# Modulation blocks of gated linear attention: eight fillers of four loads, or thirty single loads and two behind the scores of its units

## The chip, the cores and the metric

The kernel runs on one core of a Trainium2 chip. The metric is device time in microseconds (us) from one execution of the whole program. All work is single precision in and out; large products are split into a high and a low part of a narrower format (`F32R`), so that each is three matmuls.

## What is computed

Two transformer blocks, one behind the other, on 512 tokens of width 1024. What matters here lies in the first:

```python
def adaln_params(cond, w_mod, b_mod):
    return jnp.split(jax.nn.silu(cond) @ w_mod + b_mod, 6, axis=-1)
...
        sh1, sc1, gt1, sh2, sc2, gt2 = [m[:, None, :] for m in adaln_params(c, w_mod[l], b_mod[l])]
...
        qg, kg, vg, r, gf, gb = gla_inputs(px, gla_gate_up[l], gla_gate_bias[l])
        _, _, og = gla_bidir(qg, kg, vg, gf, gb, s_f, s_b)
...
        od = diff_attend(qd, jnp.concatenate([kd_c, kd], axis=2), jnp.concatenate([vd_c, vd], axis=2), lam)
        mix = jnp.concatenate([gla_merge(og, r, gla_norm_g[l]), diff_merge(od, diff_norm_g[l], lam_init)], axis=-1) @ w_out[l]
        x = x + gt1 * mix
        x = x + gt2 * swiglu(modulate(x, norm2_g[l], sh2, sc2), w_ffn_in[l], w_ffn_out[l])
```

`sh1` and `sc1` are needed at the very start. The other four modulation vectors (`gt1`, `sh2`, `sc2`, `gt2`: 4096 columns of `w_mod`, 16.8 MB) are needed only behind both attentions. The gate `r` is needed in `gla_merge`.

## The kernel before, in words

The stretch at issue has two stages. **Gated linear attention** (some 187 to 323 us of the trace) is a loop over 16 units (4 chunks of 128 tokens by 4 heads). A unit is `out_exp` (matmuls L834 to L839 that sum gates, then exponentials on ACT), `out_ops` (DVE multiplies L857 to L861 that scale queries and keys), `out_scores` (matmuls L873 to L883, copies and a masked sum on ACT and DVE up to L895) and `out_unit` (matmuls L903 and L904). The loop writes the scores of unit u, then `out_exp` and `out_ops` of unit u + 1, then `out_unit` of u. At the head of a chunk `xgates` computes the next chunk's gates (L782). **Differential attention** (some 323 to 480 us) loops over 4 heads by 4 query tiles; its first matmuls are the transposes L958, its scores L998 and L999.

Both stages have short matmuls with chains through ACT and DVE between them. To keep TensorE (PE) busy, independent work is written between them from a list, `fillers`. Each entry has a cost, and `fill_in(us)` takes entries while the time granted covers half the cost of the next. A unit grants `FG` = 4.2 us, a query tile `FA` = 3.2 us. The list holds tiles of the projections `w_dk`, `w_dv` and `w_dq` (cost 2.9, 24 matmuls L285 to L287 of 256 columns), four tiles of the gate projection `w_gr` (cost 5.5, 24 matmuls L196 to L198 of 512 columns, then a sigmoid on ACT, L147 to L149), for the memory of the second block `mem_in` (eight pieces, L1058 and on), `mem_stats`, `mem_k` and `mem_v`, and, at the places `GM` and `MM`, eight modulation blocks (cost 3.9).

A **modulation block** makes 512 of the 4096 columns. It loads 2 MB as four pieces `wm` of 512 KB (L680) and issues eight matmuls L332 (`acc<-wm,silc`), two to a piece. They have 32 output rows each, and go in turn to four strips of TensorE, so that four can run side by side. Then ACT copies the sum (L335, `mr`), four transposes follow (L338), and DVE adds up (L339, L341). Four blocks are fillers of the loop, four of differential attention.

Pieces `wm` and all weight tiles `wf` share one ring of two buffers. Weights that are loaded there (L178) leave their buffer when ACT has made the high part (L187, `whi`) and DVE the low part (L188, `wlo`); these parts have three buffers each. A `wm` leaves when its matmuls are done. All these loads are issued by SP, in order; a load that waits for its buffer holds up those behind it. Accumulators `acc` have two PSUM banks. A scheduler at build time merges the work into one fixed order for each engine; every engine then runs its list in order.

Of the kernel before, what the change touches and what calls it, by code (L numbers as in the profile page):

```python
# [10 lines left out]
F32 = mybir.dt.float32  # L11
# [8 lines left out]
KT = D // 128  # L20
# [7 lines left out]
NLEV = 7  # L28
RW = 1088
GH = 0  # L30
FA, FG, FC, A0, GM, AM, AP = 3.2, 4.2, 6.5, 2, (25, 28, 31, 34), 0, ()
PJ, FP = 10, 8
NF = 2
T0 = 1
T1 = 3
NP = 3
FS = 0.6
MM = (0, 2, 4, 6)
NR = 1
GV = 0  # L40
PL = 3
# [40 lines left out]
def kernel(ctx: ExitStack, tc: tile.TileContext, a: dict, out: bass.AP, stop=None):  # L82
    nc = tc.nc
    V, G, A, T = nc.vector, nc.gpsimd, nc.scalar, nc.tensor
# [5 lines left out]
    ring = ctx.enter_context(tc.tile_pool(name="ring", bufs=3))  # L90
# [8 lines left out]
    def acc():  # L99
        return ps.tile([128, 512], F32, tag="acc", name="acc", bufs=naccs)  # L100
# [19 lines left out]
    silc = const.tile([128, KT, 32], F32, name="silc")  # L120
# [98 lines left out]
    def fm(w, ms, nk, bhi, blo, alloc, evac, segs=FULL, lo_eng=None, after=None, keep=None, every=4,  # L219
           have=None):  # L220


        def chunk(m, k0):
            if nk == 4:
                hi, lo = wsplit(w[m // 2].rearrange("p m k c -> p (m k c)"), 1024, lo_eng, keep and keep())
                have[m + 1, 0] = hi[:, 512:], lo[:, 512:]
                return hi, lo
            kn = min(8, nk - k0)
            return wsplit(w[m, :, k0:k0 + kn, :].rearrange("p k m -> p (k m)"), kn * 128, lo_eng, keep and keep())

        have = {} if have is None else have
        for a_, b_ in segs:
            for m in ms:
                p = alloc(m)
                for k in range(nk):
                    c = (m, k // 8)
                    if c not in have:
                        have[c] = chunk(m, k // 8 * 8)
                    hi, lo = have[c]
                    sl = slice(k % 8 * 128, k % 8 * 128 + 128)  # L240
                    mm3(p[:, a_:b_], hi[:, sl], lo[:, sl], bhi(k)[:, a_:b_], blo(k)[:, a_:b_], k == 0, k == nk - 1)
                    if k % every == every - 1 and k < nk - 1:
                        step()
                evac(m, a_, b_, p[:, a_:b_])
                step()
            if len(segs) > 1:
                drain()
                if after is not None:
                    between.append(after(a_, b_))
# [71 lines left out]
    mid2 = mid.enter_context(tc.tile_pool(name="mid2", bufs=2))  # L321
    X0 = midp.tile([128, KT, S], F32, tag="a16", name="X0")

    def mod_block(m0, n, load, mpool):


        p = acc()[:, :128 * n]
        for k in range(KT):
            if k == 0 or (k - k0 + 1) * 128 * n > wf.shape[-1]:
                wf, k0 = load(k), k  # L330
            j = k % 4
            ins = T.matmul(p[32 * j:32 * j + 32, :], silc[:, k], wf[:, (k - k0) * 128 * n:(k - k0 + 1) * 128 * n],  # L332
                           start=k < 4, stop=k >= 4, skip_group_check=True, tile_position=(0, 32 * j)).ins
        mr = mpool.tile([128, 128 * n], F32, tag="mr", name="mr")
        A.copy(mr, p)  # L335
        q = acc()[:, :128 * n]
        for i in range(n):
            T.transpose(q[:, i * 128:(i + 1) * 128], mr[:, i * 128:(i + 1) * 128], ident)  # L338
        V.tensor_reduce(mods[:, m0:m0 + n], q.rearrange("p (m j r) -> p m r j", m=n, j=4)[:, :, 0:2, :], AX, ALU.add)  # L339
        o = COLS["b_mod"][0] + m0  # L340
        V.tensor_tensor(mods[:, m0:m0 + n], mods[:, m0:m0 + n],  # L341
                        cols[:, o:o + n].rearrange("p (m o) -> p m o", o=1).to_broadcast([128, n, 2]), ALU.add)
        return ins

    def affine(dst, gname, sc0, row, k0=0, kn=KT):

# [16 lines left out]
    with tc.tile_pool(name="st", bufs=1) as st, tc.tile_pool(name="st2", bufs=2) as st2:  # L363
# [84 lines left out]
        ins = mod_tiles(8)  # L448
        warm(WV, ins)
        nx = normed(X0, S, "x")  # L450
        ins = next(nx)
# [14 lines left out]
        ins = mod_tiles(10)  # L466
        for k0 in (2, 4, 6):
            ins = queued(ins, lambda: next(part))
            ins = queued(ins, lambda: mod_tiles(k0))
# [4 lines left out]
            ins = queued(ins, lambda: next(part))  # L474
            if k0 < 6:
                ins = queued(ins, lambda: mod_tiles(10 + k0))
# [5 lines left out]
        if Q3:  # L482
            ins = queued(ins, lambda: next(part))
# [5 lines left out]
        for _ in range(2 - Q3):  # L489
            ins = queued(ins, lambda: next(part))  # L490
# [65 lines left out]
    for t in range(2):  # L556
        p = acc()
# [8 lines left out]
    for dst, t0, n in ((downc[0:32, :], 0, 2), (down[0:32, 1:1 + S], 2, 4)):  # L566
        p = mis()
# [50 lines left out]
    fillers = []  # L618
# [49 lines left out]
    def silu_r(m, x, y, p):  # L668
# [2 lines left out]
        e = mid2.tile([128, S], F32, tag="sg", name="sg", bufs=1)  # L671
        sigmoid(e, p)
        V.tensor_tensor(got_rs[0][:, m], p, e, ALU.mult)
    for m in range(4):
        fillers.append((5.5, lambda m=m: fm(a["w_gr"], [m], KT, hx, hxl, accs, silu_r)))

    def mod_job(n):
        def load(k):
            t = ring.tile([128, RW], F32, tag="wf", name="wm", bufs=2)[:, :1024]
            nc.sync.dma_start(t, a["w_mod"][n, k // 4, :, k % 4:k % 4 + 2].rearrange("p k n -> p (k n)"))  # L680
            return t
        return lambda: mod_block(16 + 4 * n, 4, load, mid2)
    mod_jobs = [(3.9, mod_job(n)) for n in range(8)]
    for at in GM:
        fillers.insert(at, mod_jobs.pop(0))
    left = [0.0]
    late_by = [0]

    def fill_in(us):

        left[0] += us
        while fillers and left[0] >= 0.5 * fillers[0][0]:
            cost, run = fillers.pop(0)
            pe_late[0] = late_by[0]
            run()
            pe_late[0] = 0
            left[0] -= cost
# [43 lines left out]
    for jt in range(2):  # L741
        pe = s2()[:, :512]
        for z, ldiag in ((0, LSUF), (1, LPX)):
# [6 lines left out]
            for i, (lm, t) in enumerate(terms):  # L750
                for r, gx in enumerate(cg[t][1:]):
                    T.matmul(zsl(pe, z), Lr[:, lm], zsl(gx, z), start=i == 0 and r == 0,
                             stop=i == len(terms) - 1 and r == 1, skip_group_check=True)
# [34 lines left out]
    for c in range(TT):  # L788
# [7 lines left out]
        for h in range(4):  # L796
            T.matmul(pe[:, 512 + 32 * h:544 + 32 * h], g[:, h * 128:(h + 1) * 128], f32(Lr[:, LONE, 0:32]), start=True, stop=True,
                     skip_group_check=True)
# [26 lines left out]
    def out_exp(c, h):  # L825

        if h == GH and c < 3:
            gx[c + 1] = xgates(c + 1, 1)
        g, gh, gl = gx[c]
        hs = slice(h * 128, (h + 1) * 128)  # L830
        pe = s2()
        for j in range(4):
            b = slice(32 * j, 32 * j + 32)
            T.matmul(pe[b, 896:1024], g[:, hs][:, b], f32(Lr[:, LPRE if j < 2 else LSUF]), start=True, stop=True,  # L834
                     skip_group_check=True, tile_position=(0, 32 * j))
        for r, gx_ in enumerate((gh, gl)):
            T.matmul(pe[:, 0:512], gx_[:, hs], LT[:, 0:512], start=r == 0, stop=r == 1)
        for r, gx_ in enumerate((gh, gl)):
            T.matmul(pe[:, 512:896], gx_[:, hs], LT[:, 512:896], start=r == 0, stop=r == 1, skip_group_check=True)  # L839
        Es = []  # L840
        for hf in range(2):
            E = gt.tile([128, 4, 128], F32, tag="E", name="E", bufs=4)
            A.activation(E, pe[:, hf * 512:(hf + 1) * 512].rearrange("p (l i) -> p l i", l=4), AF.Exp)
            Es.append(E)
        return Es

    def out_ops(c, h, Es):

        ts = slice(c * 128, (c + 1) * 128)
        qb = q2[:, h, ts].rearrange("p (o i) -> p o i", o=1)  # L850
        kb = k2[:, h, ts].rearrange("p (o i) -> p o i", o=1)
        res = []
        for hf in range(2):
            nl = 4 - hf
            E = Es[hf]
            QX = gt.tile([128, 4, 128], F32, tag="QX", name="QX", bufs=3)
            V.tensor_tensor(QX[:, :nl], Rq[:, 4 * hf:4 * hf + nl], qb.to_broadcast([128, nl, 128]), ALU.mult)  # L857
            if hf:
                A.copy(QX[:, 3], q2[:, h, ts])
            V.tensor_tensor(QX, QX, E, ALU.mult)  # L860
            V.tensor_tensor(E[:, :nl], E[:, :nl], kb.to_broadcast([128, nl, 128]), ALU.mult)  # L861
            res.append((E, QX))
        return res, QX[:, 3]
# [53 lines left out]
    for u, unit in enumerate(units):  # L917
        AT = out_scores(*unit, ops[0])
        qi = ops[1]
        if u < 15:  # L920
            ops = out_ops(*units[u + 1], out_exp(*units[u + 1]))
        fill_in(FG * FS)
        out_unit(*unit, AT, qi)
        fill_in(FG * (1 - FS))
    while len(fillers) > NR:
        fillers.pop(0)[1]()
    gla_scope.close()
    qn = dq_tile()[:, 0:8].rearrange("p (t u) n -> p t (u n)", u=2)
    dv = (dq_tile()[:, 12:16], dq_tile()[:, 8:12])
# [197 lines left out]
            sl = slice(k * 128, k * 128 + 128)  # L1127
            mm3(p, w[0][:, sl], w[1][:, sl], mhi[:, k], mlo[:, k], k == 0, False)

    fillers += [mod_jobs.pop(0) for _ in range(AM)]  # L1130
    fillers.append((0.0, mix_in))
    for k in range(KT):
        fillers.append((0.0, lambda k=k: mem_in(k)))
        if k in MM:
            fillers.append(mod_jobs.pop(0))
    fillers.append((1.0, mem_stats))
    fillers += [(2.6, lambda m=m: mem_k(m)) for m in range(4)]
    fillers += [(2.6, lambda hf=hf, t=t: mem_v(hf, t)) for hf in range(2) for t in range(2)]
    fillers += [(1.0, lambda h=h: gla_merge(h)) for h in range(4)]
    for at in AP:  # L1140
        fillers.insert(at, mod_jobs.pop(0))
    fillers += mod_jobs
    fillers.append((0.0, load_x))
    left[0] = 0.0
    late_by[0] = HA
# [273 lines left out]
    for hf in range(2):  # L1419
        get = tm_load(a["w_v2"], hf, 260)  # L1420
        for t in range(TT):
            p = acc()
# [11 lines left out]
    p = mis()  # L1434
    for kt in range(TT):
        T.matmul(p[0:8, kt * 128:S], lf[:, kt], tri[:, 0:S - kt * 128], start=kt == 0, stop=kt == TT - 1,
                 skip_group_check=True)
# [397 lines left out]
```

## Time and profile before

| | |
|---|---|
| Time, median of 3 runs | 1678.38 us (1676.87 to 1685.67) |
| Profiled execution, its own time | 1687.99 us |
| Its span, first to last instruction | 1686.2 us |
| Work around the span | 1.8 us |
| PE busy | 1614.0 us (96%) |
| Mean granted TensorE clock | 0.979 |
| Loop of gated linear attention, 187.00 to 323.18 us | 136.2 us for 16 units |

The profiled execution is 9.6 us above the median, so sums made on its trace are carried over to the median as differences. A busy PE is not PE at its peak: the ends of matmuls are modelled. Idle time before an instruction is put down to what came last.

In the rows below, a stretch shows its length, the busy time of PE, PEld, DVE, ACT and POOL with their instructions, the granted clock, and the share of time and GB/s of the DMA engines. A wait shows total, times and longest. A row in order of time shows start and busy time.

### The profile page before, as it was taken

The numbers are of one execution on the slowest core, as the hardware profiler recorded it, in microseconds if no ns is written. First come the engines' busy times: TensorE is split into PE (matmuls) and PEld (weight loads), VectorE is DVE, ScalarE is ACT, GpSimd is POOL, SyncE is SP. The second block draws the span as 40 slices with busy tenths as digits, with TensorE's granted clock in tenths as the row PEclk, the third lists the DMA queues.
The fourth block names the chain that finished last, engine by engine and source line by source line (L and its number), as shares of the span: only waits on it lengthen the run. The fifth ranks groups of instructions, "written<-read, shape, count | busy, mean of one in ns | idle before, by whom it ended". The sixth has DMA issues, their size and how long they took to land.

```text
span 1686.2 us, 25313 instructions
## 1 busy us (share of the span) xinstructions
PE 1614.0 (96%) x9988; PEld 1359.6 (81%) x9988; DVE 949.1 (56%) x1728; ACT 721.4 (43%) x1374; POOL 323.4 (19%) x354
## 2 busy tenths in 40 slices
PE   9999889889999999999999999999899899999997
PEld 6898766558889888888888778888888888888886
DVE  6547876668856122223335675445677877777233
ACT  4425454457635322232233565234456544444221
POOL 1323310131112221210004000122333322221002
PEclk9999989999999999999999999999899899999999
DMA  9222134243423233333332212335111233333332
GB/s 375 67 72 76 39 111 142 82 148 94 141 63 114 75 100 100 100 91 92 96 111 75 70 38 69 94 101 175 50 29 36 76 91 97 100 91 96 101 91 73
DMA packets 47464, 161.93 MB, mean 96 GB/s; under 512 B 5488, under 2 KB 10096, under 8 KB 45552
## 3 DMA queue, kind: packets, MB, share of 16 engines
q1 hardware_dynamic: 44752, 157.74, 30.0%
q10 hardware_dynamic: 2304, 2.29, 0.4%
q8 instruction: 79, 1.29, 0.3%
q0 software_dynamic: 288, 0.28, 0.1%
q14 instruction: 41, 0.34, 0.1%
HBM read 157.41 MB, written 3.15 MB: 95 GB/s over the span
## 4 chain that ended last, share of the span: by engine, by line
PE 82%; DVE 9%; ACT 3%; DMA 2%; issue 2%; POOL 1%; SPq 0%; DVEq 0%; POOLq 0%; ACTq 0%
PE acc L197 15%; PE acc L196 15%; PE acc L198 15%; PE s L196 5%; PE s L197 5%; PE s L198 5%; PE acc L286 2%; PE acc L287 2%; PE acc L285 2%; PE acc L332 2%; DMA wm<-in_w_mod 2%; DVE wlo L188 1%; PE mis L1027 1%; PE mis L1503 1%; DVE Ym L1334 1%
## 5 line engine op out<-in xcount | busy, mean ns | idle before, releaser
L187 ACT CAST whi<-wf 128x1024 fp32r<-128x1024 f32 (+4 forms) x221 | 228.5, 1035 | 429.3 <-PE acc L197 287.6
L188 DVE TENSOR_TENSOR wlo<-wf,whi 128x1024 fp32r<-128x1024 f32 (+2 forms) x183 | 225.8, 1234 | 179.9 <-ACT whi L187 174.5
L196 PE MATMUL acc<-qhi,whi 128*128 128x512 f32 (+1 forms) x640 | 240.9, 376 | 0.0
L198 PE MATMUL acc<-qhi,wlo 128*128 128x512 f32 (+1 forms) x640 | 240.8, 376 | 0.0
L197 PE MATMUL acc<-qlo,whi 128*128 128x512 f32 (+1 forms) x640 | 240.5, 376 | 0.0
L197 PEld LDWEIGHTS acc<-qlo,whi 128*128 128x128 f32 x640 | 122.3, 191 | 20.0 <-issue 0.2
L196 PEld LDWEIGHTS acc<-qhi,whi 128*128 128x128 f32 x640 | 122.3, 191 | 19.9
L198 PEld LDWEIGHTS acc<-qhi,wlo 128*128 128x128 f32 x640 | 122.3, 191 | 19.4
L188 POOL TENSOR_TENSOR wlo<-wf,whi 128x1024 fp32r<-128x1024 f32 x38 | 91.0, 2395 | 209.5 <-ACT whi L187 209.5
L197 PE MATMUL s<-qlo,whi 128*128 128x512 f32 (+1 forms) x336 | 128.3, 382 | 0.0
L196 PE MATMUL s<-qhi,whi 128*128 128x512 f32 (+1 forms) x336 | 128.0, 381 | 0.0
L198 PE MATMUL s<-qhi,wlo 128*128 128x512 f32 (+1 forms) x336 | 127.9, 381 | 0.0
L1298 DVE TENSOR_TENSOR e<-e,s 128x512 f32<-128x512 f32 (+1 forms) x22 | 14.3, 652 | 154.0 <-PE s L198 153.8
L197 PE MATMUL acc<-glo,whi 128*128 128x512 f32 (+1 forms) x208 | 74.3, 357 | 0.1
L196 PE MATMUL acc<-ghi,whi 128*128 128x512 f32 (+1 forms) x208 | 74.4, 358 | 0.0
L198 PE MATMUL acc<-ghi,wlo 128*128 128x512 f32 (+1 forms) x208 | 74.2, 357 | 0.0
L196 PEld LDWEIGHTS s<-qhi,whi 128*128 128x128 f32 x336 | 63.9, 190 | 11.9
L198 PEld LDWEIGHTS s<-qhi,wlo 128*128 128x128 f32 x336 | 63.9, 190 | 11.8
L197 PEld LDWEIGHTS s<-qlo,whi 128*128 128x128 f32 x336 | 63.8, 190 | 11.8
L196 PE MATMUL acc<-Fhi,whi 128*128 128x512 f32 (+1 forms) x187 | 71.6, 383 | 0.0
L197 PE MATMUL acc<-Flo,whi 128*128 128x512 f32 (+1 forms) x187 | 71.5, 383 | 0.0
L198 PE MATMUL acc<-Fhi,wlo 128*128 128x512 f32 (+1 forms) x187 | 71.5, 382 | 0.0
(642 smaller groups left out, 3941.7 us busy)
## 6 DMA issues: line engine op xcount, KB each, us to landing
wf<-in_w_ffn_in SPq DMA_DIRECT2D x44, 512.0 KB, 3.6
wf<-in_w_up SPq DMA_DIRECT2D x44, 512.0 KB, 3.5
wm<-in_w_mod SPq DMA_DIRECT2D x32, 512.0 KB, 4.0
wm<-in_w_mod SPq DMA_DIRECT2D x8, 1024.0 KB, 13.5
wf<-in_w_ffn_out SPq DMA_DIRECT2D x16, 512.0 KB, 3.5
wf<-in_w_g SPq DMA_DIRECT2D x16, 512.0 KB, 3.5
wf<-in_w_down SPq DMA_DIRECT2D x16, 512.0 KB, 3.5
X<-in_xT SPq DMA_DIRECT2D x4, 1024.0 KB, 5.0
```

The costliest lines, as they stand in the source:

```text
L187: A.copy(hi[:, :n], wf[:, :n])
L188: (lo_eng or V).tensor_tensor(lo[:, :n], wf[:, :n], f32(hi[:, :n]), ALU.subtract)
L196: T.matmul(o, lhi, rhi, start=start, stop=False)
L197: T.matmul(o, lhi, rlo, start=False, stop=False)
L198: ins = T.matmul(o, llo, rhi, start=False, stop=stop).ins
L285: T.matmul(o, bhi(k), whi, start=k == 0, stop=False)
L286: T.matmul(o, bhi(k), wlo, start=False, stop=False)
L287: T.matmul(o, blo(k), whi, start=False, stop=k == KT - 1)
L332: ins = T.matmul(p[32 * j:32 * j + 32, :], silc[:, k], wf[:, (k - k0) * 128 * n:(k - k0 + 1) * 128 * n], start=k < 4, stop=k >= 4, skip_gr ...
L1027: T.matmul(p[:, :128], aT[:, kt * 128:(kt + 1) * 128], v, start=kt == 0, stop=kt == NKT - 1)
L1334: V.tensor_tensor(Y(k, x, y), Y(k, x, y), rbp, ALU.mult)
L1503: T.matmul(pO[:, ts], vz[:, kt, hp_, 64 * e:64 * e + 128], pT[:, kt * 128:(kt + 1) * 128], start=kt + e == 0, stop=kt - t + e == 1, skip_g ...
```

## The change

The eight blocks are no fillers any more. Behind the scores of each unit two calls of `mod_step` load one piece each (L689 of the changed kernel) and issue its two matmuls (L695); after four calls ACT copies the sum (L699). `mod_end`, called once in two units behind the operands of the next unit, issues the transposes and the sums (L341 to L344). So a block spans two units, and all eight are done in the loop. The time for fillers in a unit falls from 4.2 to 2.2 us, that of a query tile rises from 3.2 to 3.3 us. Of the four `w_gr` tiles two stand at the end of the loop's list, and two ahead of `mix_in` in differential attention.

```diff
-FA, FG, FC, A0, GM, AM, AP = 3.2, 4.2, 6.5, 2, (25, 28, 31, 34), 0, ()
+FA, FG, FC, A0, GR = 3.3, 2.2, 6.5, 2, 2
...
-MM = (0, 2, 4, 6)
...
-    for m in range(4):
-        fillers.append((5.5, lambda m=m: fm(a["w_gr"], [m], KT, hx, hxl, accs, silu_r)))
-
-    def mod_job(n):
-        def load(k):
-            t = ring.tile([128, RW], F32, tag="wf", name="wm", bufs=2)[:, :1024]
-            nc.sync.dma_start(t, a["w_mod"][n, k // 4, :, k % 4:k % 4 + 2].rearrange("p k n -> p (k n)"))
-            return t
-        return lambda: mod_block(16 + 4 * n, 4, load, mid2)
-    mod_jobs = [(3.9, mod_job(n)) for n in range(8)]
-    for at in GM:
-        fillers.insert(at, mod_jobs.pop(0))
+    gr_jobs = [(5.5, lambda m=m: fm(a["w_gr"], [m], KT, hx, hxl, accs, silu_r)) for m in range(4)]
+    fillers += gr_jobs[:GR]
+    def mod_step():
+        n, k0 = mod_at[0] // 4, mod_at[0] % 4 * 2
...
+        wf = ring.tile([128, RW], F32, tag="wf", name="wm", bufs=2)[:, :1024]
+        nc.sync.dma_start(wf, a["w_mod"][n, k0 // 4, :, k0 % 4:k0 % 4 + 2].rearrange("p k n -> p (k n)"))
+        if k0 == 0:
+            mod_p["p"] = acc()
+        p = mod_p["p"]
+        for k in range(k0, k0 + 2):
+            j = k % 4
+            T.matmul(p[32 * j:32 * j + 32, :], silc[:, k], wf[:, (k - k0) * 512:(k - k0 + 1) * 512],
+                     start=k < 4, stop=k >= 4, skip_group_check=True, tile_position=(0, 32 * j))
+        if k0 == 6:
+            mr = mid2.tile([128, 512], F32, tag="mr", name="mr")
+            A.copy(mr, p)
+            mod_p[n] = mr
...
         AT = out_scores(*unit, ops[0])
         qi = ops[1]
+        for _ in range(2):
+            mod_step()
         if u < 15:
             ops = out_ops(*units[u + 1], out_exp(*units[u + 1]))
+        if u % 2 == 0:
+            mod_end()
         fill_in(FG * FS)
         out_unit(*unit, AT, qi)
...
+    fillers += gr_jobs[GR:]
     fillers.append((0.0, mix_in))
     for k in range(KT):
         fillers.append((0.0, lambda k=k: mem_in(k)))
-        if k in MM:
-            fillers.append(mod_jobs.pop(0))
```

**Place 1: SP's loads ahead of and in the loop.** `wf<-in_w_dv` is a half of the weights of four tiles of `w_dv`, `wm` a modulation piece. Before, where the first block's loads begin:

```order
L178 DMA wf_2045<-in_w_dq 128x1024
L178 DMA wf_2051<-in_w_dq 128x1024
L178 DMA wf_2387<-in_w_dv 128x1024
L178 DMA wf_2393<-in_w_dv 128x1024
L680 DMA wm_2491<-in_w_mod 128x1024
L680 DMA wm_2495<-in_w_mod 128x1024
```

And where the same two weight loads stand in the changed kernel; `wm_2528` and `wm_2532` are pieces seven and eight, those of unit 3:

```order
L689 DMA wm_2528<-in_w_mod 128x1024
L689 DMA wm_2532<-in_w_mod 128x1024
L177 DMA wf_2590<-in_w_dv 128x1024
L177 DMA wf_2596<-in_w_dv 128x1024
L689 DMA wm_2669<-in_w_mod 128x1024
L689 DMA wm_2674<-in_w_mod 128x1024
```

The two halves of `w_dv` moved from ahead of the first block's pieces to behind eight pieces, and the next pieces are behind them. The second pair of `w_dv` loads stands behind ten more pieces, the first `w_gr` load behind twelve more, and the second `w_gr` load behind the last two.

**Place 2: PE where the first tile of `w_dv` begins.** `whi` and `wlo` are the parts of its weights. Before, between `out_exp` of one unit and this tile:

```order
L837 MATMUL s2_2316<-LT_1421,glx01_1967 128x512
L839 MATMUL s2_2316<-LT_1421,ghx01_1966 128x384
L839 MATMUL s2_2316<-LT_1421,glx01_1967 128x384
L287 MATMUL acc_2338<-whi_2053,hlo_88 128x256
L285 MATMUL acc_2338<-whi_2053,hhi_87 128x256
L286 MATMUL acc_2338<-wlo_2054,hhi_87 128x256
L287 MATMUL acc_2338<-whi_2053,hlo_88 128x256
L285 MATMUL acc_2399<-whi_2389,hhi_87 128x256
L286 MATMUL acc_2399<-wlo_2390,hhi_87 128x256
```

And in the changed kernel (`whi_2592` comes from the load `wf_2590` of place 1, which needs the buffer of `wm_2528`):

```order
L695 MATMUL acc_2402<-wm_2528,silc_78 32x512
L695 MATMUL acc_2402<-wm_2532,silc_78 32x512 x2
L804 MATMUL mis_2538<-gu_96,down_604 128x4x64
L856 MATMUL s2_2550<-Lr_1422,gx11_2143 32x128 x4
L859 MATMUL s2_2550<-LT_1421,ghx11_2144 128x512
L859 MATMUL s2_2550<-LT_1421,glx11_2145 128x512
L861 MATMUL s2_2550<-LT_1421,ghx11_2144 128x384
L861 MATMUL s2_2550<-LT_1421,glx11_2145 128x384
L925 MATMUL mis_2246<-gv_607,AT_2517 128x128
L926 MATMUL mis_2246<-Sst_1615,QX_2426 128x128
L284 MATMUL acc_2602<-whi_2592,hhi_87 128x256
L285 MATMUL acc_2602<-wlo_2593,hhi_87 128x256
```

Between the matmuls that free the buffer and those that need the weights loaded into it now stand nine matmul instructions in seven rows (`xgates`, `out_exp`, `out_unit`) and nothing else.

**Place 3: PE at the end of the loop.** Before, the last `w_gr` tile, the last unit, and the fifth modulation block ahead of the transposes L958 of differential attention:

```order
L198 MATMUL acc_3793<-hhi_87,wlo_3797 128x512
L903 MATMUL mis_3547<-gv_607,AT_3782 128x128
L904 MATMUL mis_3547<-Sst_1615,QX_3709 128x128
L332 MATMUL acc_3939<-wm_3940,silc_78 32x512 x2
L332 MATMUL acc_3939<-wm_3944,silc_78 32x512 x2
L332 MATMUL acc_3939<-wm_3948,silc_78 32x512 x2
L958 MATMUL mis_3871<-identr_76,sgt_3868 128x128 x4
```

In the changed kernel (`acc_3998` is the second `w_gr` tile, whose load needs the buffer of `wm_3808`):

```order
L197 MATMUL acc_3730<-hhi_87,wlo_3734 128x512
L695 MATMUL acc_3692<-wm_3808,silc_78 32x512
L695 MATMUL acc_3692<-wm_3812,silc_78 32x512 x2
L925 MATMUL mis_3545<-gv_607,AT_3797 128x128
L926 MATMUL mis_3545<-Sst_1615,QX_3716 128x128
L341 MATMUL acc_3836<-ident_75,mr_3816 128x128 x4
L195 MATMUL acc_3998<-hhi_87,whi_4001 128x512
L196 MATMUL acc_3998<-hlo_88,whi_4001 128x512
L197 MATMUL acc_3998<-hhi_87,wlo_4002 128x512
```

The last block ends in the loop, and 72 matmuls of three `w_gr` tiles, 18 of them ahead of the first transposes, stand where four blocks stood.

## Rows read from the trace of the kernel before

**Rows 1.** The page: busy time of each engine.

```profile
PE 1614.0 (96%) x9988; PEld 1359.6 (81%) x9988; DVE 949.1 (56%) x1728; ACT 721.4 (43%) x1374; POOL 323.4 (19%) x354
```

**Rows 2.** Busy time by stretch: loop, start of differential attention, what follows.

```profile
187.00:323.18 136.18, 120.32 (x1597) 91.44 (x1597) 101.58 (x223) 64.82 (x178) 13.60 (x14) 0.94 0.29 94
323.18:345.00 21.82, 14.90 (x71) 6.86 (x70) 12.73 (x31) 8.71 (x20) 11.05 (x21) 0.77 0.48 150
345.00:390.00 45.00, 40.68 (x234) 27.14 (x235) 31.22 (x79) 28.08 (x66) 10.38 (x18) 0.92 0.50 154
```

**Rows 3.** What PE waited for, 186 to 323 us: total, times, longest.

```profile
PE s L873 <- DVE E L861: 6.2, 4, 4.4
PE acc L332 <- DMA wm<-in_w_mod: 3.0, 5, 2.0
PE mis L903 <- DVE AT L895: 2.8, 3, 1.3
PE acc L338 <- ACT mr L335: 2.7, 4, 0.7
PE s L883 <- DVE E L861: 0.8, 1, 0.8
```

**Rows 4.** The same in differential attention, 323.18 to 480 us.

```profile
PE acc L332 <- DMA wm<-in_w_mod: 7.4, 3, 4.1
```

**Rows 5.** Busy time in six stretches at half clock: the longest, and their sum.

```profile
326.50:333.40 6.90, 5.09 (x18) 1.65 (x18) 2.79 (x7) 1.09 (x2) 2.66 (x6) 0.51 0.65 221
...
sum 27.30, PE 24.82 PEld 15.12 DVE 14.20 ACT 7.45 POOL 7.55; mean PE 4.14 PEld 2.52 DVE 2.37 ACT 1.24 POOL 1.26
```

**Rows 6.** PE in order of time (a matmul is two records): modulation matmuls.

```profile
358.27 1.06 PE L332 MATMUL acc<-wm,silc 128*32 128x512 f32 x6
359.26 0.36 PE L958 MATMUL mis<-identr,sgt 128*128 128x128 f32 x2
...
360.02 1.04 PE L332 MATMUL acc<-wm,silc 128*32 128x512 f32 x2
361.00 0.50 PE L998 MATMUL s<-KA,QB 128*128 128x512 f32 x1
```

**Rows 7.** PE: first and last of a `w_gr` tile's 24 matmuls.

```profile
289.09 0.39 PE L196 MATMUL acc<-hhi,whi 128*128 128x512 f32 x1
...
294.30 0.39 PE L198 MATMUL acc<-hhi,wlo 128*128 128x512 f32 x1
```

**Rows 8.** PE: one block's first pair of pieces, then its third and fourth.

```profile
274.88 1.07 PE L332 MATMUL acc<-wm,silc 128*32 128x512 f32 x8
...
280.10 1.05 PE L332 MATMUL acc<-wm,silc 128*32 128x512 f32 x4 [0.24 <-DMA wm<-in_w_mod]
281.39 1.05 PE L332 MATMUL acc<-wm,silc 128*32 128x512 f32 x4 [0.24 <-DMA wm<-in_w_mod]
```

**Rows 9.** The page's costliest groups: the two parts of loaded weights.

```profile
L187 ACT CAST whi<-wf 128x1024 fp32r<-128x1024 f32 (+4 forms) x221 | 228.5, 1035 | 429.3 <-PE acc L197 287.6
L188 DVE TENSOR_TENSOR wlo<-wf,whi 128x1024 fp32r<-128x1024 f32 (+2 forms) x183 | 225.8, 1234 | 179.9 <-ACT whi L187 174.5
```

**Rows 10.** SP in order of time: the second `w_dv` load ahead of the loop.

```profile
179.92 0.33 SPq L178 DMA_DIRECT2D wf<-in_w_dv  x1
```

**Rows 11.** PE in order of time: `out_unit`, `xgates`, and `out_exp` up to the next scores.

```profile
236.40 0.49 PE L903 MATMUL mis<-gv,AT 128*128 128x128 f32 x2
...
236.95 1.03 PE L782 MATMUL mis<-gu,down 128*128 128x256 f32 x4
237.81 0.45 PE L873 MATMUL s<-QX,E 128*128 128x128 f32 x2
...
238.45 0.41 PE L834 MATMUL s<-Lr,gx 128*32 128x128 f32 x8
...
239.61 0.40 PE L883 MATMUL s<-QX,E 128*32 128x32 f32 x24
```

**Rows 12.** Loads `mk` of the memory: issue to landing.

```profile
DMA to landing us min/median/max: 2.4/2.5/4.9
```

More of the change, by code (lines that the diff above doesn't have):

```diff
@@ L335, in mod_block, with mod_sums @@
         A.copy(mr, p)
+        mod_sums(m0, n, mr)
+        return ins
+    def mod_sums(m0, n, mr):
         q = acc()[:, :128 * n]
@@ L342, in mod_block @@
                         cols[:, o:o + n].rearrange("p (m o) -> p m o", o=1).to_broadcast([128, n, 2]), ALU.add)
-        return ins
     def affine(dst, gname, sc0, row, k0=0, kn=KT):
@@ L673, in silu_r, with mod_end @@
         V.tensor_tensor(got_rs[0][:, m], p, e, ALU.mult)
-    for m in range(4):
-        fillers.append((5.5, lambda m=m: fm(a["w_gr"], [m], KT, hx, hxl, accs, silu_r)))
-    def mod_job(n):
-        def load(k):
-            t = ring.tile([128, RW], F32, tag="wf", name="wm", bufs=2)[:, :1024]
-            nc.sync.dma_start(t, a["w_mod"][n, k // 4, :, k % 4:k % 4 + 2].rearrange("p k n -> p (k n)"))
-            return t
-        return lambda: mod_block(16 + 4 * n, 4, load, mid2)
-    mod_jobs = [(3.9, mod_job(n)) for n in range(8)]
-    for at in GM:
-        fillers.insert(at, mod_jobs.pop(0))
+    gr_jobs = [(5.5, lambda m=m: fm(a["w_gr"], [m], KT, hx, hxl, accs, silu_r)) for m in range(4)]
+    fillers += gr_jobs[:GR]
+    mod_at = [0]
+    mod_p = {}
+    def mod_step():
+        n, k0 = mod_at[0] // 4, mod_at[0] % 4 * 2
+        if n == 8:
+            return
+        mod_at[0] += 1
+        wf = ring.tile([128, RW], F32, tag="wf", name="wm", bufs=2)[:, :1024]
[11 more added lines that the diff above has]
+            mod_p[n] = mr
+    def mod_end():
+        n = mod_at[0] // 4 - 1
+        mr = mod_p.pop(n, None)
+        if mr is not None:
+            mod_sums(16 + 4 * n, 4, mr)
     left = [0.0]
@@ L926 @@
         fillers.pop(0)[1]()
+    mod_end()
     gla_scope.close()
@@ L1128, in out_part @@
             mm3(p, w[0][:, sl], w[1][:, sl], mhi[:, k], mlo[:, k], k == 0, False)
-    fillers += [mod_jobs.pop(0) for _ in range(AM)]
+    fillers += gr_jobs[GR:]
     fillers.append((0.0, mix_in))
@@ L1139 @@
     fillers += [(1.0, lambda h=h: gla_merge(h)) for h in range(4)]
-    for at in AP:
-        fillers.insert(at, mod_jobs.pop(0))
-    fillers += mod_jobs
     fillers.append((0.0, load_x))
```

## The prediction

> **What bounds the kernel now.** I read the page's busy times first: PE works 96% of the span [rows 1], so a change gains only what PE does not have to do, or does not have to wait for. Next the busy time by stretch [rows 2]. In the loop PE is busy 120.3 of 136.2 us and no other engine over 102, so PE leads there too; 16 idle us are to be had, and a unit takes 136.2 / 16 = 8.5 us. The start of differential attention is worse: 14.9 of 21.8 us busy, at a mean clock of 0.77. Third, what PE waited for, of at least the length that the view lists: 15.5 us in the loop [rows 3], of which 9.8 are for DVE (4.4 of them one wait at the loop's head), and 7.4 us for modulation pieces in attention [rows 4]. Last, the granted clock: six stretches stand at the lower level, 1.2 GHz, together 27.3 us with PE busy 24.8 [rows 5]. Each contains or follows block matmuls or a wait of over 1 us. At the full level the same work would take half, so they cost 24.8 / 2 = 12.4 us, about 2.1 each.
>
> The reader is to see that the eight blocks cost their matmuls, 13.1 us of waits, and perhaps most of the 12.4 us of clock. The change can touch no more than that.
>
> **The change part by part.**
>
> *The block matmuls* (A). There are as many as before, but cut up otherwise. What counts is the number of separate groups on PE: three matmuls side by side took 359.26 - 358.27 = 0.99 us and a single one 361.00 - 360.02 = 0.98 [rows 6]. In the fixed orders I count 24 groups before and 27 after (one or two per unit, as the builder merged them). Three more cost 2.9 us. Bounds: 0 if neighbours overlap, 5.9 if all three fall into the low clock.
>
> *Waits removed* (B). The blocks' waits for pieces go, 3.0 [rows 3] and 7.4 [rows 4], because a piece now has most of a unit to arrive. The transposes' wait for the copy `mr`, 2.7 [rows 3], goes too, since they stand a unit's operands behind it. Together -13.1.
>
> *The gate tiles* (C). 24 matmuls took 294.30 - 289.09 + 0.2 = 5.4 us at full clock [rows 7]. Two tiles leave the loop, by the builder's order even three, and they are done in attention instead. This is PE work at one price on either side: 0. Their sigmoids go to ACT in attention, which was busy 28 of 45 us [rows 2], so it has room.
>
> *Weights that now come just in time* (D). This is the term that I think decides. Pieces and weights share two buffers, and SP issues in order. Before, the second `w_dv` load was issued at 179.92, ahead of the loop [rows 10], while its tile began some 25 us later. After, it is issued only when a piece of unit 3 has been consumed, and PE needs it 3 us on (place 2 above). How long the round takes is seen in a block: from the first pair of pieces to the matmuls of the pieces that reuse their buffers took 280.10 - 274.88 = 5.2 us, and 281.39 - 274.88 = 6.5 us for the second buffer [rows 8]. A weight then needs its high part on ACT, 1.04 us, and its low part on DVE, 1.23 us [rows 9]: ready 6.2 and 7.5 us after the freeing matmul. At place 2 the work between is the group itself (0.98), `xgates` (0.4), `out_exp` with what surrounds it (239.61 - 238.45 + 0.2 = 1.3) and `out_unit` (236.95 - 236.40 = 0.55) [rows 11]: 3.3 us. So PE stands 2.9 us for the high part, 1.1 for the low one (it arrives 1.3 later, behind one short matmul), and some 0.6 for the second half: 4.6. At the second `w_dv` pair a third of the next unit's scores stands between as well, about 2 us: 4.6 - 2.0 = 2.6. The first `w_gr` tile has scores between and one load only: 1.3. At the second (place 3) there is the group, `out_unit` and the four transposes, 2.2 us in all, so 6.2 - 2.2 = 4.0 and 0.8 for the low part: 4.8. Sum +13.3. Behind the cast that waits for its load stand, on ACT, the exponentials of the next unit, which DVE and then PE wait for, so such a wait does not end with the weight. Bounds: 0 if the scheduler's other work covers it, 20 if the exponentials add another half.
>
> *Units without filler* (E). With 2.2 us granted, two units (5 to 6 and 13 to 14) have no tile between one pair of pieces and the next. Their pieces arrive 5.2 us after the freeing matmul, and PE gets there after some 3.2 and 2.7: 2.0 + 2.5 = +4.5. Bounds: 0, if PE waits for DVE's operands there anyway, to 9.
>
> *DVE waits* (F). 9.8 - 4.4 = 5.4 us [rows 3]. With PE late by D and E, about half should find DVE done: -3. Bounds: -5.4 to +5, since with fewer tiles between scores DVE's chain is less covered.
>
> *Clock* (G). The six low stretches belonged to the blocks and go: -12.4 [rows 5]. But D and E make six new waits of over 1 us, and the six old stretches behind such waits cost 2.1 each: +12.4. I take 0; bounds -12.4 and +14. The Trainium skill says (TensorE: Matmul & The Clock Gate, HAM oscillation) that a loop whose compute is shorter than the wait for its next load starts every tile cold. The trace agrees as far as it goes: the low stretches lie at the blocks, 0.51 granted in the longest [rows 5].
>
> *Attention* (H). Without the blocks the start fills with gate tiles, and small waits on POOL and ACT lose perhaps 2. Against that all eight memory pieces now stand in a row, and their loads are bunched: the six `mk` loads behind the first pair come in three rounds, each 2.5 us from issue to landing [rows 12], with conversions 3.5 to 4.5 us, against some 13.7 us of PE work that stands between. Hidden on paper, +2 for a late one (0 to +8). Together 0.
>
> Sum: 2.9 - 13.1 + 0 + 13.3 + 4.5 - 3 + 0 + 0 = **+4.6**. On the profiled execution that is 1688.0 + 4.6 = 1692.6; that execution is 9.6 above the median shown, so on the median 1678.4 + 4.6 = 1683.0. A difference of 0.5% (8.4 us) is about what a measurement of this kernel can tell from no change; this is less.
>
> **The rivals.**
>
> *Two buffers hide it (faster).* Each pair of pieces has a whole unit of 8.5 us, and the round is 5.2 to 6.5 us [rows 2, 8]. If loads are issued earlier than I place them, because PE runs late elsewhere, then D and E vanish (-17.8) and F's 3 us come back. The sum is 2.9 - 13.1 = -10.2, with half of the clock's gain -16.4, with all of it -22.6: 1668, 1662 or 1656. For it: the pieces' rate, 1.05 MB in 8.5 us, is 123 GB/s, and the longest low stretch moved 221 [rows 5]. Against it: the four weight loads that stand between two pairs of pieces, with 3.3 us where 6.2 are needed. The Trainium skill's rule to double-buffer so that loads overlap with compute (Trainium Kernel Development and Optimization, Best Practices) would give this outcome; no run here shows two buffers to be enough for three uses.
>
> *The loop stays at the low clock (slower).* Before, eight blocks had six low stretches. After, every one of 16 units has short 32-row groups and most of them a wait. A low stretch costs 2.1 [rows 5]; two more than I count bring the result past +8.4, and eight more give 4.6 + 16.5 = +21: 1699. For it: every one of the six stretches lies at such matmuls or waits. Against it: one group alone, with dense scores around it, is shorter than the groups of four before.
>
> *The memory becomes the bound (slower).* If the row of eight memory pieces, no longer spaced out by blocks, makes PE wait a round or two for `mk`, H is +8 and not 0: 1691. For it: the bunching. Against it: 13.7 us of cover.
>
> **How the numbers follow.** Forecast, 0.46, by itself 1672 to 1694 (D from 6 to 20 with G within 5): 0.04 faster, 0.32 same, 0.10 slower. Buffers hide it, 0.25: 0.24 faster, 0.01 same. Low clock, 0.18: 0.03 same, 0.15 slower. Memory, 0.11: 0.05 same, 0.06 slower. Faster by over 0.5% 0.28, within 0.41, slower 0.31. The range goes from 1662, the middle of the first rival (0.12 below), to 1697, just short of the second's end (0.08 above).
>
> **What would show it right or wrong.** In the changed profile's list of waits, PE's modulation matmuls should wait for no piece in attention; instead PE should wait for `whi` and `wlo` of `w_dv` and `w_gr` at four places, 2 to 5 us each, and for `wm` at two units. The mean clock of the loop should be near the 0.94 of before [rows 2], the start of attention clearly above its 0.77, and the loop's length nearly as before although 11 to 16 us of gate tiles have left it. If those `whi` waits are absent, D is wrong and the first rival holds. If the loop's clock is below 0.9 the second holds. If PE waits for `mk` or the memory's parts over 5 us, the third.

## The result and the profile after

The changed kernel takes 1697.5 us (median of 7 runs, 1694.5 to 1702.3) and the kernel before, beside it, 1682.1 us: a ratio of 1.0092, with a 95% interval of 1.0072 to 1.0113. It is slower by some 15 us where I had forecast 5, and lies just outside the range (1697). Its profiled execution took 1698.3 us, with a span of 1696.5. The profiled execution of the kernel before took 1688.0 us, at a mean granted clock of 0.979 where the 95 executions timed beside the experiments had 0.980 to 0.989, so the two traces differ by 10.3 us only.

The page's busy times of the changed kernel, which answer to [rows 1]:

```profile
PE 1618.3 (95%) x9988; PEld 1364.1 (80%) x9988; DVE 955.1 (56%) x1728; ACT 723.2 (43%) x1374; POOL 327.3 (19%) x354
```

PE has 4 us more of busy time, and more idle time. Where, is shown by stretches: the loop, the first 21.8 us of differential attention, the rest of the gate tiles, the stretch from the memory's first conversion to its statistics, and the rest of attention. The last two rows are of another answer of the same view, over the eight stretches at half clock from 190 to 412 us: the longest, and the sum of all.

```profile
187.00:326.10 139.10, 122.76 (x1601) 84.96 (x1600) 99.56 (x223) 60.73 (x171) 13.15 (x14) 0.91 0.41 134
326.10:347.90 21.80, 16.18 (x65) 11.97 (x64) 13.21 (x24) 11.16 (x19) 8.76 (x14) 0.74 0.50 157
347.90:376.00 28.10, 27.81 (x163) 22.79 (x162) 22.18 (x47) 19.39 (x44) 3.42 (x8) 0.95 0.07 20
376.00:407.00 31.00, 20.60 (x125) 16.85 (x124) 24.11 (x49) 18.69 (x43) 13.31 (x17) 0.86 0.18 52
407.00:482.00 75.00, 70.92 (x512) 63.51 (x512) 52.78 (x106) 50.77 (x122) 15.04 (x17) 0.97 0.29 95
...
398.46:412.11 13.65, 8.12 (x37) 7.19 (x38) 5.44 (x14) 5.59 (x12) 3.26 (x6) 0.51 0.32 103
sum 51.20, PE 43.57 PEld 34.23 DVE 31.78 ACT 16.37 POOL 10.10; mean PE 5.45 PEld 4.28 DVE 3.97 ACT 2.05 POOL 1.26
```

The loop grew by 2.9 us, to 139.1, against 136.2 in [rows 2]. The start of attention has a clock of 0.74 and not, as forecast, one clearly above the 0.77 of before. Attention as a whole, from the loop's end to its last transposes, took 144.9 us before (323.18 to 468.10) and takes 155.9 now. Behind attention 3.6 us come back, which makes the 10.3 between the traces. Most of the 11 us lie in one place: from 376 to 407 us PE is busy 20.6 of 31.0. What it waits for there is in the list of waits. Rows up to the first line of dots are of the loop, the others of attention:

```profile
PE acc L695 <- DMA wm<-in_w_mod: 4.3, 4, 1.9
PE s L895 <- DVE E L883: 3.3, 2, 1.9
PE acc L284 <- DVE kg L605: 2.2, 1, 2.2
PE mis L925 <- ACT AT L917: 1.7, 5, 0.6
PE acc L284 <- ACT whi L186: 1.4, 1, 1.4
PE mis L925 <- DVE AT L917: 1.3, 2, 1.1
PE acc L285 <- DVE wlo L187: 1.1, 1, 1.1
PE acc L284 <- DVE mods L342: 0.7, 2, 0.4
...
PE acc L196 <- DVE mlo L1087: 4.1, 4, 1.6
PE mis L310 <- DVE r_m L169: 3.4, 1, 3.4
PE acc L195 <- ACT whi L186: 3.4, 1, 3.4
PE s L1025 <- ACT p L1031: 2.9, 4, 1.3
PE acc L195 <- ACT mhi L1086: 1.7, 2, 1.5
```

The loop's waits are those that the forecast named. Attention's are new: `mlo`, `r_m` and `mhi`, together 9.2 us, are the parts of the memory and its statistics, for which the list of the kernel before shows no wait. PE and ACT, in order of time, show why. First PE: the last matmul of the last gate tile, and the first of the memory.

```profile
374.15 0.39 PE L197 MATMUL acc<-hhi,wlo 128*128 128x512 f32 x1
...
377.04 0.28 PE L195 MATMUL acc<-mhi,whi 128*128 128x256 f32 x1
```

Then ACT: the memory's loads `mk`, and the first and last of the eight conversions.

```profile
334.17 0.82 ACTq L1085 DMA_DIRECT2D mk<-in_memT  x2
...
376.18 0.51 ACT L1086 ACTIVATE mhi<-mk,cols 128x256 fp32r<-128x256 f32 x1
...
382.22 0.34 ACTq L1085 DMA_DIRECT2D mk<-in_memT  x1
...
396.27 0.33 ACTq L1085 DMA_DIRECT2D mk<-in_memT  x1
399.33 0.51 ACT L1086 ACTIVATE mhi<-mk,cols 128x256 fp32r<-128x256 f32 x1 [1.49 <-DMA mk<-in_memT]
```

The loads of two pieces of the memory were issued at 334 us, and the first conversion ran 42 us later, at 376.18, 2 us behind the start of the gate tile's last matmul. Only then could a third load have a buffer. The reason is in the code, and I had not looked at it:

```python
mhi = hp.tile([128, KT, S], F32R, tag="hhi", name="mhi")
mlo = hp.tile([128, KT, S], F32R, tag="hlo", name="mlo")
mnh = mhi[:, 4:8].rearrange("p k (u t) -> p (k u) t", u=2)
```

The memory's parts are written into the buffers of `hhi` and `hlo`, the inputs of all the projections, and `hp` has one buffer for each. Before, the last reader of `hhi` was the last gate tile in the loop, at 322.42; the first conversion came at 333.91 and PE's first memory matmul at 383.34, so the chain had 49 us:

```profile
322.42 0.39 PE L198 MATMUL acc<-hhi,wlo 128*128 128x512 f32 x1
...
333.91 0.51 ACT L1059 ACTIVATE mhi<-mk,cols 128x256 fp32r<-128x256 f32 x1
...
383.34 0.38 PE L196 MATMUL acc<-mhi,whi 128*128 128x256 f32 x1
```

After, the gate tiles spread over attention read `hhi` until 374, and the chain had 0.9 us.

Two theories were put to the test. **Buffer theory:** the moved gate tiles hold `hhi`, the memory's chain loses its cover, and that is the loss. **Loop theory:** the loss is that of the loop and the start of attention, where just-in-time loads, waits and the low clock came with the blocks, and the memory's waits only take their place.

### The profile page after: what moved, and what is told of

It is laid out like the page before. It is cut to its first block, busy times and chain, and to the rows that moved or that the text cites. A ratio compares the mean times of both kernels' runs of the same rounds, so it can differ in the third digit from the quotient of the medians.

```text
span 1696.5 us, 25334 instructions
## 1 busy us (share of the span) xinstructions
PE 1618.3 (95%) x9988; PEld 1364.1 (80%) x9988; DVE 955.1 (56%) x1728; ACT 723.2 (43%) x1374; POOL 327.3 (19%) x354
```

## The experiments

All were timed in five rounds beside the kernel before, whose median was 1681 to 1682 us. A ratio is to that kernel, with its 95% interval. Kernels with other data give wrong gates and are good for timing alone.

**Other data for the gate tiles.** The three gate tiles behind the loop read a small tile of their own.

```diff
-    gr_jobs = [(5.5, lambda m=m: fm(a["w_gr"], [m], KT, hx, hxl, accs, silu_r)) for m in range(4)]
+    zt = []
+    gr_jobs = [(5.5, lambda m=m: fm(a["w_gr"], [m], KT, hx if m == 0 else lambda k: zt[0], hxl if m == 0 else lambda k: zt[0],
+                                    accs, silu_r)) for m in range(4)]
...
+    zt.append(ap2.tile([128, S], F32R, name="zt", bufs=1))
+    G.memset(f32(zt[0]), 0.5)
```

> The changed kernel, but the three gate tiles in differential attention multiply a small constant tile in place of hhi and hlo, so that they cost PE the same and no longer hold the buffers that the memory's parts mhi and mlo are written to; two heads' gates come out as something else. Buffer theory (the gate tiles keep hhi until 374.5 us, so the memory's chain starts 40 us late and has no cover: 10 us of waits and 4 of clock): 1681 to 1687 us, PE's waits for the memory's mlo, mhi and r_m below 2 us together, and no stretch of 13.6 us at half clock. Loop theory (the waits for weights and pieces in the loop and the low clock there make the loss): still 1694 to 1699 us.

1687.6 us, ratio 1.0032 (1.0019 to 1.0044): 10 us of the 15 are gone, just short of what was expected, and no wait for `mlo`, `mhi` or `r_m` is left in the list. The gate tiles are written ahead of the memory's pieces here as in the change, and still the first conversion came at 335.6 us and the first memory matmul at 385.0, so it was the buffer that held the conversions and not their place in the list:

```profile
L1090 ACT ACTIVATE mhi<-mk,cols x8: 495/510/523, 335.6 to 363.5; 128x256 fp32r<-128x256 f32 x8
...
384.95 0.28 PE L195 MATMUL acc<-mhi,whi 128*128 128x256 f32 x1
```

The stretch of 13.7 us at half clock stayed, but at another place (329 us), where PE waited 7.9 us for the new tile:

```profile
PE acc L195 <- POOL zt L964: 7.9, 1, 7.9
```

**The same, with the tile set by DVE** (`V.memset`).

> As the kernel whose attention gate tiles multiply a constant tile, but that tile is set by DVE instead of POOL, where it waited 7.9 us behind other work; two heads' gates are left wrong in the same way. Buffer theory: with that wait gone too, 1676 to 1684 us, so that the whole loss of the change is the hold on hhi. Loop theory: 1687 us or more, since the loop's waits and low clock remain.

1685.4 us, 1.0021 (1.0003 to 1.0040), between what the two theories expected. The wait did not go: 7.8 us, now with no releaser shown. In both traces the tile is set right behind `og` (L936), which ends gated linear attention: at 331.8 us by POOL, at 332.5 by DVE. That the space for the tile becomes free only there would explain this; it was not tried apart.

**The same, for the last two gate tiles only** (`m < 2` in place of `m == 0`), so that PE does not wait for the constant.

> The changed kernel, where only the last two gate tiles multiply the constant tile in place of hhi and hlo (two heads' gates are wrong); the first of the three keeps its data, so that PE does not wait for the constant at the start as it did for 7.8 us. hhi is then free some 30 us earlier than in the change. Buffer theory: 1677 to 1684 us, no waits of over 1 us for mlo, mhi, msq or r_m. Loop theory: 1686 us or more even without these waits.

1687.6 us, 1.0034 (1.0018 to 1.0050), a miss for the buffer theory, where the loop theory had put it. The conversions ran from 343.0 us, and of the memory's waits one of 1.4 us for `msq` remained. So three kernels without the hold, or with most of it gone, lie 10 to 12 us below the change, and by their ratios 3.5 to 5.7 us above the kernel before. The first part is the buffer's; the second is not. In two of the three the wait of nearly 8 us for the constant is a cost of the experiment.

**Only the gate tiles moved, in the kernel before.**

```diff
-FA, FG, FC, A0, GM, AM, AP = 3.2, 4.2, 6.5, 2, (25, 28, 31, 34), 0, ()
+FA, FG, FC, A0, GM, AM, AP = 3.8, 3.2, 6.5, 2, (25, 28, 31, 34), 0, ()
...
+    fillers += gr_jobs[:2]
...
+    fillers += gr_jobs[2:]
     fillers += [mod_jobs.pop(0) for _ in range(AM)]
```

> The kernel before with the gate tiles alone moved: the same three tiles behind the loop, all eight blocks fillers as before, a unit granted 3.2 us and a query tile 3.8. Buffer theory: slower than before by 8 to 14 us (1690 to 1696), with waits for mlo, mhi or r_m of 5 us or more, since the memory's parts wait for the last gate tile here too. Loop theory: no block stands behind scores, so within 4 us of before (1678 to 1686).

1684.7 us, 1.0013 (1.0002 to 1.0025), a miss for the buffer theory as I had put it. `hhi` was held until 373.5 us here too, and the wait was there, in one piece:

```profile
PE mis L293 <- POOL msq L1069: 5.1, 1, 5.1
```

But the blocks still stood among attention's fillers, so the first memory matmul came at 396.5, 22 us behind the first conversion. In this kernel the hold cost little; in the change nothing was left to put behind it.

**All gate tiles in the loop, blocks as in the change** (`FG, GR = 3.5, 4`).

> The changed kernel with all four gate tiles in the loop (GR 4, a unit granted 3.5 us): blocks behind scores as in the change, hhi free when the loop ends. Buffer theory: faster than the change by 7 to 14 us (1683 to 1690), the memory's chain starting some 40 us earlier, with perhaps some 3 us of waits for it at the start of attention, where it has little cover. Loop theory: 1694 to 1699 us, or more, since the loop has more just-in-time weights.

1707.5 us, 1.0142 (1.0125 to 1.0158), 10 us slower than the change: the clearest miss, and the loop theory's side. PE waited little for the memory, 3.9 us, but in the loop it waited 10.9 us for `E` instead of 3.3, and attention began with nothing to cover its own start-up. The first row is of the loop, the others of attention:

```profile
PE s L895 <- DVE E L883: 10.9, 6, 2.7
...
PE mis L985 <- issue: 8.0, 1, 8.0
PE s L1025 <- ACT p L1031: 4.8, 5, 2.8
```

From 350.2 us on, 17.1 us were at half clock. The gate tiles had not only held a buffer, they had also covered that start. Nor did the chain start 40 us earlier: the memory's loads were issued at 354.9 us, 12 us behind the last reader of `hhi`, and the first conversion at 358.8 waited for its load.

**More time granted at the start of attention** (`A0 = 12`), and **one gate tile more in the loop** (`FG, GR = 2.55, 3`).

> The changed kernel with 12 us instead of 2 granted at the start of differential attention (A0), so that the gate tiles run there and not between the query tiles. Buffer theory: the last gate tile and the first memory conversion come 10 to 20 us sooner than the 374 and 376 us of the change, and the time falls by 4 to 10 us, to 1688 to 1693. Loop theory, or the memory's loads by themselves as the bound: no change, 1694 to 1700.

> The changed kernel with one gate tile more in the loop (GR 3, a unit granted 2.55 us); a tile and a third stay behind it as cover for the start of attention. Buffer theory: 5 to 12 us faster than the change (1686 to 1692). If the start of attention needs all three tiles as cover, as the kernel with none there lost 24 us, it is no faster: 1695 to 1702.

The first: 1697.1 us, 1.0099 (1.0068 to 1.0130), no change, a miss for the buffer theory as put. `hhi` came free at 366, 8 us sooner, but the memory's matmuls moved up as well, to 367.4, and PE still waited 8.0 us for the memory (with 1.2 for `msq` and 1.0 for `mlo`):

```profile
PE mis L310 <- DVE r_m L169: 3.0, 1, 3.0
PE acc L195 <- ACT mhi L1086: 2.8, 4, 1.2
```

The second: 1691.9 us, 1.0063 (1.0037 to 1.0088), as expected, though the first memory matmul still stood only 1.1 us behind the first conversion.

**Four buffers for the memory's loads** (`tag="mk", bufs=4`).

> The changed kernel with four buffers instead of two for the memory's loads mk; the gate tiles still hold hhi until some 374 us. If the loss is that six of eight loads are issued only after hhi is free, in rounds of two: four loads lie ready, two rounds fewer, and the time falls by 3 to 8 us (1689 to 1694), with the eight conversions done in 12 to 16 us instead of 23. If hhi alone counts (the conversions and sums behind it, whatever the loads do): no change, 1695 to 1700.

1693.6 us, 1.0070 (1.0044 to 1.0097): some 4 us less than the change, as forecast, but the intervals overlap. The trace shows the step. The conversions in the view of tile `mk`:

```profile
L1086 ACT ACTIVATE mhi<-mk,cols x8: 494/502/512, 375.3 to 390.3; 128x256 fp32r<-128x256 f32 x8
```

From first to last 15 us, against 23 in the change, as forecast. So the rounds of loads are probably a part of the cost, where `hhi` holds them up.

**Half of the change.** Four blocks behind scores, one step in a unit; the others fillers of attention as before; all gate tiles in the loop.

```diff
-FA, FG, FC, A0, GR = 3.3, 2.2, 6.5, 2, 2
+FA, FG, FC, A0, GR = 3.2, 3.2, 6.5, 2, 4
...
-        for _ in range(2):
-            mod_step()
+        mod_step()
...
+        if k in (0, 2, 4, 6):
+            fillers.append(mod_jobs.pop(0))
```

> Half of the change: four blocks behind scores, one step in each unit (a unit granted 3.2 us), the other four blocks fillers in attention as before, all gate tiles in the loop. Buffer theory: within 4 us of before (1678 to 1686). Loop theory: half of the loss, 1687 to 1692 us.

1679.6 us, 0.9984 (0.9970 to 0.9998): slightly faster than before, as the buffer theory expected. No stretch of the loop was at half clock.

**Six blocks** behind scores, two in attention, and the **half with four buffers** for `mk`.

> As the kernel with four blocks behind scores, but six: three steps in two units, two blocks left as fillers of attention, all gate tiles in the loop's list. If blocks behind scores cost nothing by themselves: 1677 to 1684 us, near the half. If each of them costs the loop more than it saves: 1686 us or more.

> Half of the change (four blocks behind scores, four as fillers of attention, gate tiles in the loop) with four buffers for mk. The memory's chain had 49 us of cover there already and PE did not wait for it: no difference from the half with two buffers, 1677 to 1682 us. If the loads of the memory also set the start of attention there, 2 to 4 us less.

Six: 1684.0 us, 1.0022 (1.0001 to 1.0042), at the upper end of what was expected. The half with four buffers: 1685.2 us, 1.0017 (1.0002 to 1.0033), slower than the half with two where I had expected no difference. Its list of waits differs in small ones (`nb` 2.2, `X` 2.7 us); what in the order brought them is open. The 5.6 us between these two halves, of which none was expected, are as much as the smaller differences here, so a ratio within 0.3% of 1 says little about its cause by itself.

**The half with a gate tile as cover** (`FG = 2.8`): one tile and a third stand behind the loop.

> The half again (four blocks behind scores, four as fillers of attention), but a unit is granted 2.8 us instead of 3.2, so that the last gate tile and a third of another stand behind the loop as cover for the start of attention, where the half waited 7.1 us for the first filler block's pieces. Buffer theory: the four blocks still stand between the memory's conversions and its matmuls, so holding hhi a tile longer costs nothing; the pieces arrive behind the gate tiles: 1674 to 1680 us, waits for pieces below 4 us. If any gate tile behind the loop costs by holding hhi: 1684 us or more, with waits for mlo, msq or r_m.

1678.0 us, 0.9972 (0.9958 to 0.9986), as expected: faster than both kernels. The pieces for which the half waited 7.1 us at the start of attention now arrive behind the gate tiles. First that wait in the half, then the largest wait from 300 us on in this kernel, and that for pieces:

```profile
PE acc L331 <- DMA wm<-in_w_mod: 7.1, 3, 4.0
...
PE s L1031 <- ACT p L1037: 3.1, 3, 2.3
...
PE acc L331 <- DMA wm<-in_w_mod: 0.6, 1, 0.6
```

Put side by side, with the time from the first conversion to PE's first memory matmul read from each trace in order of time, and the granted clock as the mean of all executions:

| kernel | blocks behind scores | first conversion | first memory matmul | between | ratio | mean granted clock |
|---|---|---|---|---|---|---|
| half, a gate tile as cover | 4 | 331.0 | 386.6 | 55.6 | 0.9972 | 0.987 |
| before | 0 | 333.9 | 383.3 | 49.4 | 1 | 0.985 |
| other data, set by POOL | 8 | 335.6 | 385.0 | 49.4 | 1.0032 | 0.979 |
| half | 4 | 327.1 | 376.4 | 49.3 | 0.9984 | 0.986 |
| half, four buffers for `mk` | 4 | 326.8 | 376.1 | 49.3 | 1.0017 | 0.984 |
| other data, set by DVE | 8 | 336.9 | 385.7 | 48.8 | 1.0021 | 0.981 |
| six behind scores | 6 | 336.5 | 366.6 | 30.1 | 1.0022 | 0.985 |
| other data, last two | 8 | 343.0 | 370.6 | 27.6 | 1.0034 | 0.981 |
| before, gate tiles moved | 0 | 374.4 | 396.5 | 22.1 | 1.0013 | 0.985 |
| three gate tiles in the loop | 8 | 357.8 | 358.9 | 1.1 | 1.0063 | 0.982 |
| the change | 8 | 376.2 | 377.0 | 0.9 | 1.0092 | 0.978 |
| four buffers for `mk` | 8 | 375.3 | 376.1 | 0.8 | 1.0070 | 0.980 |
| all gate tiles in the loop | 8 | 358.8 | 359.4 | 0.6 | 1.0142 | 0.977 |
| gate tiles first | 8 | 366.8 | 367.4 | 0.5 | 1.0099 | 0.978 |

With 22 us or more of other work between, no kernel is over 1.0034; with 1 us none is below 1.0063. The date at which `hhi` comes free does not order them. All kernels with 1 us have eight blocks behind scores, so what shows the part of the cover by itself is the rows with eight: 1.0021 to 1.0034 with 27 us or more, 1.0063 to 1.0142 with 1 us. The clock goes with the blocks: 0.977 to 0.982 with eight, 0.984 to 0.987 with fewer, whatever the cover. So neither theory explains all of it.

## Why the prediction was wrong

The step that failed is **H**, attention, taken as 0 with "Hidden on paper, +2 for a late one (0 to +8)". It counted the loads' rounds and "some 13.7 us of PE work that stands between", and assumed that the conversions could start as soon as a piece had landed. They could not: the gate tiles that term C moved at "one price on either side" read the very buffers into which the conversions write. C was right about PE and blind to what the tiles hold. The term measured about 10 us by the kernels with other data (1.0092 to 1.0032, 1.0021 and 1.0034: 10, 12 and 10 us). In the trace it is 10.4 idle us between 376 and 407, plus 8.12 / 2 = 4.1 for the stretch at half clock that went with them, of which some would be lost in any case. By the prediction's own sign, over 5 us of waits for the memory's parts, the third rival holds: the waits for `mlo`, `r_m` and `mhi` were 9.2. That rival named +8; the place was right, and the mechanism (blocks that space the pieces out) was not: with all of them in the loop and the hold removed, PE hardly waited.

The rest of the sum, +4.6, came out near what is left: without the hold the change stood 3.5 to 5.7 us above the kernel before. That is luck, since its terms are off both ways: D is 7.4 us too high, F some 4.6 too low, and G too low. For D, place 2 in the changed kernel: the last freeing matmuls, the high part on ACT, and the matmul that needs it.

```profile
214.46 1.05 PE L695 MATMUL acc<-wm,silc 128*32 128x512 f32 x5
...
219.63 1.03 ACT L186 CAST whi<-wf 128x1024 fp32r<-128x1024 f32 x1
...
220.72 0.58 PE L284 MATMUL acc<-whi,hhi 128*128 128x256 f32 x1 [1.39 <-ACT whi L186]
```

The terms one by one:

- **A** (+2.9) cannot be read apart from the clock. PE's busy time rose by 4.3 us in all, and in low stretches the matmuls took longer: those of 512 columns 0.63 us and more in the stretch from 330 us, 0.39 at 374 us.
- **B** (-13.1) is right as far as it goes: no piece is waited for in attention, and no transpose waits for `mr`, [rows 3, 4]. The waits for pieces that remain, all in the loop, are counted in E.
- **D** (+13.3) was more than twice what was measured. The mechanism held at place 2: the last freeing matmuls at 214.46 us, the high part done at 219.63 + 1.03 = 220.66, 6.2 us behind them, as [rows 8, 9] gave. But PE lost 1.4 and 1.1 us for the weights there, since it had already waited 1.1 for DVE, and 3.4 at place 3 where 4.8 was forecast. At the second `w_dv` pair and the first `w_gr` tile it did not wait for weights. Waits with one cause ahead of them were added as if each stood alone. Together 5.9. (Eleven matmul instructions in eight rows stand at place 2, not nine in seven; the sum was made from times and does not depend on it.)
- **E** (+4.5) measured 4.3, at four places instead of two.
- **F** (-3) went the other way: 7.0 us for `E`, `AT` and `mods` in the loop, 5.4 before.
- **G** (0): from 187 to 412 us low stretches with PE busy 43.6 us against 30.8 before (seven stretches, the six of [rows 5] and one at the loop's head), so (43.6 - 30.8) / 2 = +6.4, within its bounds. 4.1 of it is the memory's, and so a consequence of H. The loop's clock was 0.91, not "near the 0.94". And this is too little, because the trace before stands at 0.979: over all executions the mean granted clock is 0.978 for the change and 0.985 for the kernel before. The same kernel before took 1676.5 us in an execution at 0.989 and 1687.8 us in one at 0.980. On that scale, an estimate, the 0.007 between the kernels go with some 9 of the 15 us. The three kernels without the hold stand 0.004 to 0.006 below the kernel before, some 5 to 7 us, as much as their whole loss. What comes first there, the waits or the low clock, is not shown.

The first rival, two buffers that hide all, fell with the waits for `whi`. The second, a loop that stays at low clock, is not what happened at four blocks (no low stretch in the loop) and only partly at eight (0.91). The loop theory has a share: by their ratios -2.7 us at four blocks behind scores, +3.7 at six, 3.5 to 5.7 at eight without the hold. At eight it goes with the clock; at six, where the clock is that of the kernel before, it does not. Which waits make it was not separated.

## What to carry to other kernels

When a step is moved later, list not only what it computes and loads but every buffer that it reads: the next stage may write into one of them, and then starts when the moved step ends. Cover is a distance, from the producer's start to its first consumer, and it is spent when work that stood between them is moved elsewhere; freeing the producer sooner gained nothing in the kernel where the consumer moved up with it (1.0099). Moving half of the work and leaving the other half as cover beat both the old place and the new one, by 0.2 and 0.3% against the old; the half with four buffers for `mk` did not (1.0017). And a trace is one execution: before clock terms are read off it, its granted clock is to be set beside that of the other executions.

## What the runs showed of the hardware that I had not expected

Low-clock stretches were long where short waits followed each other. In the change 13.65 us stood at 0.51 around the memory's chain, with PE busy 8.1 of them; before the clock fell PE had waited five times between 385 and 397 us, for 0.2 to 1.6 us each, for DVE and ACT. In the kernel with the gate tiles first 20.5 us stood at the lower level there. The Trainium skill (TensorE: Matmul & The Clock Gate, HAM oscillation) tells of waits for loads that throttle a loop again and again. Here a fall is seen behind waits for DVE and ACT; that they brought it about is not shown.
